# A projection with rotary embedding: when stores are issued, and two more tile pairs that take the block path

## The chip, the cores and the metric

The kernel runs on one core of one Trainium2 chip. The time is device microseconds of one execution of the whole program; lower is better. A profile is one further execution, with the hardware profiler on.

## The reference

`x` is 16 x 512 x 768, `weight` 768 x 768, `cos` and `sin` 512 x 64, all float32; there are 12 heads of 64.

```python
y = np.matmul(x, weight)
y = y.reshape(batch, seq, n_heads, head_dim)
y1, y2 = y[..., :head_dim // 2], y[..., head_dim // 2:]
...
out1 = y1 * cos1 - y2 * sin1
out2 = y2 * cos2 + y1 * sin2
out = np.concatenate([out1, out2], axis=-1)
```

So it is one matrix product of 8192 rows by 768 x 768, and on each head a rotation by the row's position. 25.17 MB of `x` are read and 25.17 MB of `out` written.

## The kernel before, in words

**Tiles and groups.** The rows are cut into 64 tiles of 128 rows, and these into 16 groups of 4 tiles. A group takes the rows of one residue of the position modulo 4 from four batches, so that one slice of cos and sin serves it. A group's result, 128 x 3072, is computed in PSUM in three units of 1024 columns (two banks each, six banks in all), which cut across the tiles: unit 0 is done a third into the group's second tile, unit 1 two thirds into the third, unit 2 at the end of the fourth. The last two groups use units of 512 or 256 columns.

**A tile's way.** TensorE needs the tile's x transposed, in float16. There are two ways:

- *Plain*: SP loads 384 KB (`load`, L189), ScalarE casts it (`cast`, xc<-xs), TensorE transposes six 128 x 128 chunks into PSUM, and ScalarE copies them out (`turn`, L232 and xt<-pt).
- *Block*: two neighbouring tiles, a pair (g, 0) or (g, 1) of group g, are loaded as four quarters of 192 KB (`load_quarter`, L201), quarters 0 and 1 by SP and 2 and 3 by ScalarE's queue; ScalarE casts the pair in one instruction (`cast_pair`, xd<-xb), and VectorE turns it by one stream transpose (`turn_pair`, L252). TensorE does no transposes for it. `BLOCKS` (L135) names the pairs that go this way: 17 before.

Twelve matmuls (L291) then make the tile's 768 output columns. When a unit of 1024 columns is complete, VectorE multiplies it by cos and by sin in one instruction (`rope`, L309, into one of five product buffers: three `tq`, and two in the space of the raw weights, which the profile calls `w_raw`), and POOL adds the halves into the group's output buffer (L320). There are four output buffers `ov`, so group g + 4 writes where group g's result was.

**What sets the order.** All instructions are put out by one Python loop over the tiles, and each engine runs its own in that order; a small class, `Flow`, adds the semaphore waits that reads and writes call for. A step waits with everything behind it on its engine, and a DMA issue holds its issuing engine in the same way. At tile i the loop (L499 to L522) puts out, in this order: the tile's matmuls, with `rope` after the piece that completes a unit; stream transposes of pairs up to 6 tiles ahead (3 for the first tiles: L511, `SETTLED` is 8); TensorE transposes up to 3 tiles ahead; casts up to 7 tiles ahead (3 or 4 for the first); then a store, if one is due. Within `casts`, ScalarE also issues quarters 2 and 3 of a pair some 12 tiles ahead (`LEAD`, L462), and `pump` gives SP its next loads, in the order of `fetch` (L363 to L366), as long as one of 11 row buffers, or one of 4 pair buffers, is free. A pair's cast goes into one of two buffers xd.

**Stores.** A group's output leaves in two halves of 768 KB. Half 0 of group g - 1 is issued at the first tile of group g, half 1 at the third (L514 to L517): from ScalarE's queue up to group 12, from SP's queue for groups 13 and 14. The last group's output goes in smaller pieces as its adds end.

The functions as they stand:

Of the kernel before, what the change touches and what calls it, by code (L numbers as in the profile page):

```python
# [16 lines left out]
class Flow:  # L17
# [24 lines left out]
    def do(self, e, make, reads=(), writes=(), dma=None, tick=True):  # L42
        need = {}
        for k in reads:
            for s, v in self.wrote.get(k, {}).items():
                need[s] = max(need.get(s, 0), v)
        for k in writes:
            for d in (self.wrote, self.readby):
                for s, v in d.get(k, {}).items():
                    need[s] = max(need.get(s, 0), v)  # L50
        if e == "pe":
            need.pop("pe", None)
        waits = self.settle(e, need)
        for s, v in waits[:-1]:
            self.eng[e].wait_ge(self.sem(s), v)
        i = make(self.eng[e])
        if waits:
            s, v = waits[-1]
            i.wait_op(self.sem(s), v, "sem-ge")
        name, step = (dma, 16) if dma else (e, 1)  # L60
        self.sem(name)
        at = self.count[name] + step
        if tick or dma:
            i.then_inc(self.sems[name], step)
            self.count[name] = at
            self.known[name, at] = dict(self.seen[e])
        for k in reads:
            d = self.readby.setdefault(k, {})
            d[name] = max(d.get(name, 0), at)
        for k in writes:  # L70
            self.wrote[k] = {name: at}
            self.readby[k] = {}
        return i
# [30 lines left out]
def kernel(  # L104
# [15 lines left out]
    B, S, H = x.shape  # L120
# [7 lines left out]
    QB = 4  # L128
# [3 lines left out]
    LAST = NG - 1  # L132


    BLOCKS = {(g, 1) for g in range(3, 15)} | {(g, 0) for g in (5, 7, 9, 11, 13)}  # L135

    def sbuf(name, shape, dt):
        return nc.alloc_sbuf_tensor(name, shape, dt).ap()
# [33 lines left out]
    def where(i):  # L172
        g, s = divmod(i, QB)
        return QB * (g // SB) + s, g % SB

    def pair_of(i):
        return i // QB, (i % QB) // 2

    def is_block(i):
        return pair_of(i) in BLOCKS  # L180

# [63 lines left out]
    def turn_pair(gh):  # L245
        g, h = gh
        z = ring("xp", NXP)
        dst = xp_b[z].bitcast(FP32)
        c = xc[gh]
        src, rd = xd_b[c].bitcast(FP32), [f"xd{c}"]  # L250
        v = xp_b[z].rearrange("p (t m e) -> p t e m", t=NT, e=2)
        do("dve", lambda eng: eng.transpose(out=dst, in_=src), reads=rd, writes=[f"xp{z}"])  # L252
        for s in (0, 1):
            xT[g * QB + 2 * h + s] = (
                lambda t, e, s=s: v[:, t, e, ts(s, P)], f"xp{z}")
# [3 lines left out]
    def units(g):  # L259
        if g < LAST - 1:  # L260
            return [(c, c + 1024, py[:, c : c + 1024], [f"ps{c // 512}", f"ps{c // 512 + 1}"], "pool")
                    for c in (0, 1024, 2048)]
        u = [(c, c + 512, py[:, c : c + 512], [f"ps{c // 512}"], "pool")
             for c in range(0, 3072 if g < LAST else 1536, 512)]
        if g == LAST:
            for k, (home, bank) in enumerate([
                (py[:, 1536:1792], "ps3"), (py[:, 0:256], "ps0"),
                (py[:, 2048:2304], "ps4"), (py[:, 2560:2816], "ps5"),
                (pt_b[0][:, 0:256], "pt0"), (pt_b[1][:, 0:256], "pt1"),
            ]):  # L270
                c = 1536 + 256 * k
                u.append((c, c + 256, home, [bank], "pool" if k < 3 else "dve"))
        return u

    def pieces(g, s):

        out_, lo = [], s * H
        for c0, c1, ps, banks, _ in units(g):
            step = 512 if len(banks) > 1 else c1 - c0
            for k, b in enumerate(banks):  # L280
                a, z = max(lo, c0 + k * step), min(lo + H, c0 + (k + 1) * step)
                if a < z:
                    out_.append((a, z, ps[:, a - c0 : z - c0], b))
        return out_

    def mm_piece(i, piece, c, start, stop, tick):
        g, s = divmod(i, QB)
        a, z, ps, bank = piece
        get, key = xT[i]
        t, h = c  # L290
        do("pe", lambda eng: eng.matmul(  # L291
            ps, get(t, h), w_sb[:, t, h, a - s * H : z - s * H], start=start, stop=stop),
            reads=[key, f"w{t}{h}"], writes=[bank], tick=tick)
# [37 lines left out]
    def store(g, c0, c1, e):  # L331

        o = ov_of[g]
        b, r = where(g * QB)
        s0, s1 = c0 // H, -(-c1 // H)
        dst = out.rearrange("b (p r) h -> r p b h", r=SB)[r, :, b + s0 : b + s1]
        src = ov_b[o].rearrange("p (b h) -> p b h", b=QB)[:, s0:s1]
        if (c1 - c0) % H:
            dst = dst[:, 0, c0 - s0 * H : c1 - s0 * H]
            src = src[:, 0, c0 - s0 * H : c1 - s0 * H]  # L340
        do(e, lambda eng: eng.dma_start(out=dst, in_=src),  # L341
           reads=[f"ov{o}c{c}" for c in range(c0, c1, 64)], dma=f"ov{o}_{c0}")
# [20 lines left out]
    want = [(i, i) for i in range(QB, NTILE) if not is_block(i)]  # L363
    for g, h in BLOCKS:
        want += [(g * QB + 2 * h - 2.5 + 3 * q, ((g, h), q)) for q in (0, 1)]
# [78 lines left out]
    state = {"cast": 4, "turn": 4, "bturn": 0, "half": 0}  # L444
    pairs = sorted(BLOCKS)

    def casts(upto):
        while state["cast"] < min(upto, NTILE):
            i = state["cast"]
            state["cast"] += 1  # L450
            if not is_block(i):
                castx(i, "act")
            elif i % 2 == 0:
                cast_pair(pair_of(i))
                xb_used[0] += 1
            pump()
            if state["half"] < 2 * len(pairs):
                n, q = divmod(state["half"], 2)
                g, h = pairs[n]
                if n < xb_used[0] + NB and i >= g * QB + 2 * h - LEAD:  # L460
                    load_quarter(pairs[n], 2 + q, "act")
                    state["half"] += 1  # L462

    def turns(upto):
        while state["turn"] < min(upto, NTILE):
            i = state["turn"]
            state["turn"] += 1
            if not is_block(i):
                turn(i, "act")

    def bturns(upto):
        while state["bturn"] < len(pairs):
            gh = pairs[state["bturn"]]
            if gh[0] * QB + 2 * gh[1] >= upto:
                return
            turn_pair(gh)
            state["bturn"] += 1

    C_AHEAD, T_AHEAD, B_AHEAD = 7, 3, 6
    LEAD = 12  # L480
    SETTLED = 2 * QB
# [14 lines left out]
    rope(0, U0[2])  # L496
    turns(6)

    for i in range(QB, NTILE):  # L499
        g, s = divmod(i, QB)  # L500
        us = units(g)
        done_to = (s + 1) * H
        for p in pieces(g, s):
            a, z, _, bank = p
            for c in CHUNKS:
                mm_piece(i, p, c, c == CHUNKS[0], c == CHUNKS[-1],
                         tick=c == CHUNKS[-1])
            for u in us:
                if u[1] == z:
                    rope(g, u)  # L510
        bturns(i + (B_AHEAD if i >= SETTLED else 3))  # L511
        turns(i + 1 + (T_AHEAD if i > QB + 1 else 2))
        casts(i + 1 + (C_AHEAD if i >= SETTLED else 3 if i == QB else 4))
        if s == 0 and g > 0:  # L514
            store(g - 1, 0, 2 * H, "sp" if g > LAST - 2 else "act")
        if s == 2 and g > 0:
            store(g - 1, 2 * H, 4 * H, "sp" if g > LAST - 2 else "act")  # L517
        if g == LAST:
            if s == 2:
                store(g, 0, H, "sp")  # L520
            if s == 3:
                store(g, H, 2 * H, "act")  # L522
# [43 lines left out]
```

## Time and profile before

| | us |
|---|---|
| median of 3 runs | 154.24 |
| the 3 runs | 152.16, 154.24, 154.43 |
| the profiled execution, its own time | 152.54 |
| span of the profile, first to last instruction | 150.8 |
| TensorE busy (matmuls and transposes) | 140.7 |
| VectorE busy | 129.1 |
| POOL busy | 112.9 |
| ScalarE busy | 74.8 |
| moved by DMA | 53.11 MB, 352 GB/s over the span |

PE is TensorE, PEld its weight loads, DVE VectorE, ACT ScalarE, POOL GpSimd, SP SyncE; a q behind an engine's name is its queue of DMA issues. In the rows of slices a digit is the busy share of a fortieth of the span in tenths. In the chain of work a row has start, length and the step that the end of the program depended on at that time; x36 counts instructions that were merged. In a wait row the engine, its waiting step and what released it are followed by the total, the number of times and the longest. In the timeline a row has start, length, engine, line, operation, what it writes and reads, shape and count, and in brackets the idle time of the engine before it with what ended it. Stores are ACTq or SPq rows with `out_dram<-ov`, at L341. A DMA issue's row is the time that the queue was held, and not the transfer; for a single issue, the DMA view limited to its moment gives the time to landing.

### The profile page before, as it was taken

What the parts mean: (1) busy time and instruction counts of PE and PEld (TensorE: products, weight loads), DVE (VectorE), ACT (ScalarE), POOL (GpSimd) and SP (SyncE); (2) the same over time, 40 slices, a digit from 0 to 9 for tenths busy, and PEclk for the clock granted to TensorE, in tenths of its full rate; (3) what the DMA queues carried; (4) which work ended last, traced back from release to release, by engine and by line L of the source; (5) the groups of instructions that cost most, each with busy time, mean ns of one, the idle gap of its engine ahead of it and who ended that gap; (6) DMA issues with size and microseconds to landing.
All of it is one profiled execution on the core that took longest, in us unless ns stands there. A gap on an engine that the chain in (4) does not pass through costs nothing.

```text
span 150.8 us, 2454 instructions
## 1 busy us (share of the span) xinstructions
PE 140.7 (93%) x972; PEld 86.9 (58%) x972; DVE 129.1 (86%) x88; ACT 74.8 (50%) x76; POOL 112.9 (75%) x60
## 2 busy tenths in 40 slices
PE   6669999999999999999999999899999999999950
PEld 2335666566666666555665666455666666666740
DVE  0334999677998999999989999899989999998890
ACT  3444778885863380844453372744784408342100
POOL 1000299866897889878989789878988698999970
PEclk9999999999999999999999999999999999999995
DMA  4999999999999999999999999999999999695574
GB/s 129 351 402 398 404 340 286 324 363 303 372 379 406 387 383 378 342 396 390 394 358 399 387 385 390 386 389 391 382 400 406 416 414 397 242 353 216 218 283 153
DMA packets 33147, 53.11 MB, mean 352 GB/s; under 512 B 2288, under 2 KB 20464, under 8 KB 33136
## 3 DMA queue, kind: packets, MB, share of 16 engines
q10 hardware_dynamic: 16752, 27.79, 50.1%
q1 hardware_dynamic: 16384, 25.17, 47.1%
q8 instruction: 7, 0.11, 0.3%
q14 instruction: 4, 0.03, 0.1%
HBM read 27.79 MB, written 25.17 MB: 351 GB/s over the span
## 4 chain that ended last, share of the span: by engine, by line
PE 74%; DVE 6%; ACT 5%; DMA 5%; ACTq 3%; POOL 2%; SPq 1%; issue 1%; DVEq 0%; POOLq 0%
PE py L291 68%; PE pt L232 5%; DMA w_raw<-in_weight_dram 5%; DVE w_raw L309 3%; ACTq L341 2%; ACT xd L169 2%; ACT xc L169 2%; POOL ov L320 2%; ACT xt L169 1%; ACTq L201 1%; DVE xs L309 1%; SPq L189 1%; DVE ov L320 1%; SPq L208 1%; DVE w_sb L169 0%
## 5 line engine op out<-in xcount | busy, mean ns | idle before, releaser
L320 POOL TENSOR_TENSOR ov<-tq 128x1024 f32<-128x1024 f32 (+2 forms) x33 | 69.1, 2109 | 27.9 <-DVE tq L309 27.8
L291 PE MATMUL py<-w_sb,xp 128*128 128x512 f16 (+1 forms) x408 | 69.4, 326 | 0.0
L309 DVE TENSOR_TENSOR tq<-py,csn 128x2048 f32<-128x2048 f32 (+2 forms) x33 | 65.8, 2017 | 4.0 <-PE py L291 3.6
L291 PE MATMUL py<-w_sb,xt 128*128 128x256 f16 (+1 forms) x360 | 61.2, 322 | 2.2 <-DVE w_sb L169 1.6
L291 PEld LDWEIGHTS py<-w_sb,xp 128*128 128x128 f16 x408 | 39.3, 98 | 24.6
L291 PEld LDWEIGHTS py<-w_sb,xt 128*128 128x128 f16 x360 | 33.9, 98 | 24.4 <-DVE w_sb L169 3.1
L320 POOL TENSOR_TENSOR ov<-w_raw 128x1024 f32<-128x1024 f32 (+2 forms) x21 | 43.6, 2086 | 4.6 <-DVE w_raw L309 4.5
L309 DVE TENSOR_TENSOR w_raw<-py,csn 128x2048 f32<-128x2048 f32 (+2 forms) x21 | 42.0, 1998 | 2.7 <-PE py L291 2.0
L169 ACT COPY xt<-pt 128x768 f16<-128x768 f16 x28 | 22.3, 801 | 32.9 <-PE pt L232 26.7
L169 ACT CAST xc<-xs 128x768 f16<-128x768 f32 x30 | 26.2, 903 | 20.6 <-issue 8.3
L169 ACT CAST xd<-xb 128x1536 f16<-128x1536 f32 x17 | 27.7, 1628 | 10.9 <-DVE xp L252 5.2
L252 DVE STREAM_TRANSPOSE xp<-xd 128x768 f32<-128x768 f32 x17 | 16.4, 966 | 1.1 <-ACT xd L169 1.0
L232 PE MATMUL pt<-ident,xc 128*128 128x128 f16 x180 | 15.0, 219 | 0.9 <-ACT xc L169 0.9
L232 PEld LDWEIGHTS pt<-ident,xc 128*128 128x128 f16 x180 | 12.2, 98 | 5.7 <-ACT xc L169 2.5
L169 DVE CAST w_sb<-w_raw 128x768 f16<-128x768 f32 x6 | 3.4, 560 | 4.2 <-DMA w_raw<-in_weight_dram 4.1
L394 PE MATMUL py<-cold 128*128 128x512 f16 x12 | 4.3, 513 | 1.4 <-DVE cold L345 1.4
L169 DVE COPY xt<-pt 128x768 f16<-128x768 f16 x2 | 1.1, 558 | 4.8 <-PE pt L232 4.8
L394 PEld LDWEIGHTS py<-cold 128*128 128x128 f16 x12 | 1.4, 127 | 3.3 <-issue 1.8
L169 ACT ACT_TABLE_LOAD x1 | 1.3, 1283 | 0.9 <-SPq L114 0.9
L291 PE MATMUL pt<-w_sb,xt 128*128 128x256 f16 x12 | 1.5, 272 | 0.0
L309 DVE TENSOR_TENSOR xs<-pt,csn 128x512 f32<-128x512 f32 x2 | 1.3, 682 | 0.0
L291 PEld LDWEIGHTS pt<-w_sb,xt 128*128 128x128 f16 x12 | 1.2, 98 | 0.1
(11 smaller groups left out, 3.4 us busy)
## 6 DMA issues: line engine op xcount, KB each, us to landing
out_dram<-ov ACTq DMA_DIRECT2D x26, 768.0 KB, 13.5
xs<-in_x_dram SPq DMA_DIRECT2D x30, 384.0 KB, 10.4
xb<-in_x_dram SPq DMA_DIRECT2D x34, 192.0 KB, 9.0
xb<-in_x_dram ACTq DMA_DIRECT2D x34, 192.0 KB, 10.7
out_dram<-ov SPq DMA_DIRECT2D x4, 768.0 KB, 3.4
w_raw<-in_weight_dram SPq DMA_DIRECT2D x6, 384.0 KB, 7.4
out_dram<-ov SPq DMA_DIRECT2D x1, 384.0 KB, 2.3
out_dram<-ov ACTq DMA_DIRECT2D x1, 384.0 KB, 2.3
```

The source lines that it names most:

```text
L169: eng.copy(out=o, in_=i_) if e == "act" else eng.tensor_copy(out=o, in_=i_)
L189: do(e, lambda eng: eng.dma_start(out=xs_b[k], in_=x[b].rearrange("(p r) h -> r p h", r=SB)[r]), writes=[f"xs{k}"], dma=f"xs{k}")
L201: do(e, lambda eng: eng.dma_start(out=dst[ts(q, R)], in_=src[r, q]), writes=[f"xb{k}q{q}"], dma=f"xb{k}")
L208: do(e, lambda eng: eng.dma_start(out=w_raw[:, t, h], in_=wv[t, h]), writes=[f"wr{t}{h}"], dma=f"w{t}{h}")
L232: do("pe", lambda eng: eng.transpose(pt[:, t, h, :], src[:, t, h, :], ident), reads=[f"xc{c}", "ident"], writes=[f"pt{k}"], tick=(t, h) == ...
L252: do("dve", lambda eng: eng.transpose(out=dst, in_=src), reads=rd, writes=[f"xp{z}"])
L291: do("pe", lambda eng: eng.matmul(ps, get(t, h), w_sb[:, t, h, a - s * H : z - s * H], start=start, stop=stop), reads=[key, f"w{t}{h}"], w ...
L309: do("dve", lambda eng: eng.tensor_tensor(out=tq.rearrange("p j (h d) -> p j h d", d=D), in0=ps.rearrange("p (h d) -> p h d", d=D) .unsque ...
L320: do(adder, lambda eng: eng.tensor_tensor(out=ov_b[o][:, ds(c0, w)].rearrange("p (h t d) -> p h t d", t=2, d=HD), in0=tq[:, 0].rearrange(" ...
L341: do(e, lambda eng: eng.dma_start(out=dst, in_=src), reads=[f"ov{o}c{c}" for c in range(c0, c1, 64)], dma=f"ov{o}_{c0}")
L394: do("pe", lambda eng: eng.matmul(py[:, ts(b, 512)], cold[:, 0:P], cold, start=True, stop=warmed[0] < WARM - 6), reads=["cold"], writes=[f ...
```

## The change

Three edits. `BLOCKS` gains the pairs (2, 1) and (3, 0), that is tiles 10, 11, 12 and 13: nineteen pairs. The stores of groups 0 to 10 are put out at the first and third tile of the second group after them instead of the next one; the four halves of groups 11 and 12 at the four tiles of group 13; groups 13 and 14 as before. The queue that issues each stays what it was. And at tile 8 the stream transposes look 3 tiles ahead instead of 6: the cast of (3, 0) is put out only after that point, at the end of tile 8.

```diff
-    BLOCKS = {(g, 1) for g in range(3, 15)} | {(g, 0) for g in (5, 7, 9, 11, 13)}
+    BLOCKS = {(g, 1) for g in range(2, 15)} | {(g, 0) for g in (3, 5, 7, 9, 11, 13)}
...
+    STORES = {}
+    for o in range(LAST):
+        for k in (0, 1):
+            if o < LAST - 4:
+                at = QB * (o + 2) + 2 * k
+            elif o < LAST - 2:
+                at = QB * (LAST - 2) + 2 * (o - LAST + 4) + k
+            else:
+                at = QB * (o + 1) + 2 * k
+            STORES[at] = (o, k)
...
-        bturns(i + (B_AHEAD if i >= SETTLED else 3))
+        bturns(i + (B_AHEAD if i > SETTLED else 3))
         turns(i + 1 + (T_AHEAD if i > QB + 1 else 2))
         casts(i + 1 + (C_AHEAD if i >= SETTLED else 3 if i == QB else 4))
-        if s == 0 and g > 0:
-            store(g - 1, 0, 2 * H, "sp" if g > LAST - 2 else "act")
-        if s == 2 and g > 0:
-            store(g - 1, 2 * H, 4 * H, "sp" if g > LAST - 2 else "act")
+        if i in STORES:
+            o, k = STORES[i]
+            store(o, 2 * H * k, 2 * H * (k + 1), "sp" if o > LAST - 3 else "act")
```

## The prediction

> **What bounds the kernel now.** I read the page's engine rows first, then its slices, then the chain of work that ended last, then the timeline at the two places that the change touches, and the DMA view by stretches.
>
> ```profile
> PE 140.7 (93%) x972; PEld 86.9 (58%) x972; DVE 129.1 (86%) x88; ACT 74.8 (50%) x76; POOL 112.9 (75%) x60
> PEclk9999999999999999999999999999999999999995
> DMA  4999999999999999999999999999999999695574
> ```
>
> TensorE is busy 93% of the span at a granted clock of 0.99, and the DMA engines are as full until slice 34. So either could be the limit; the chain decides.
>
> ```profile
> 44.03 13.65 PE py L291 x84
> 57.68 0.34 PE pt L232 x6
> 58.01 1.95 PE py L291 x12
> ...
> 84.15 2.37 POOL ov L320
> 86.53 1.23 ACTq L341
> ...
> 92.18 1.67 ACTq L341
> 93.85 0.04 issue
> 93.89 0.80 ACT xt L169
> 94.69 1.51 ACT xd L169
> ...
> 96.63 0.81 ACT xt L169
> 97.43 0.05 issue
> 97.48 9.92 PE py L291 x60
> ```
>
> From about 11 us to 143 us the chain is TensorE back to back: 13.65 / 7 = 1.95 us for a tile's 12 matmuls and 0.34 us (0.335 between tile starts) more after each tile that is followed by six transposes. It leaves TensorE once. There a store on ScalarE's queue waits for POOL's add, its issue and a later one take 1.23 and 1.67 us, and the copy of tile 41's xT behind them comes late: that tile starts 2.58 us after tile 40, 0.63 more than 1.95. Tile 33 starts 2.18 after tile 32, 0.23 too late, for the same queue. All other steps from tile 13 to 61 are within 0.02 us of 1.95 or 2.285.
>
> The waits of ScalarE between 44 and 118 us show how its in-order queue is held by stores:
>
> ```profile
> ACT xc L169 <- issue: 8.3, 3, 3.7
> ACT xc L169 <- POOL ov L320: 4.9, 2, 2.9
> ACT xd L169 <- issue: 2.3, 2, 1.9
> ```
>
> "issue" is a cast behind a DMA that the queue took long to accept (one store issue took 3.48 us from 69.31).
>
> **The change, part by part.** Its own time is 152.54 us, 150.8 of it span. The three plain runs are 152.16, 154.24 and 154.43; so the profiled one is 1.1% below their median, and I do the sum on it.
>
> *Four tiles lose their TensorE transposes.* Tiles 10 to 13, as pairs (2,1) and (3,0). They were four sets after tiles 7, 8, 9 and 10, where the timeline shows TensorE without a gap:
>
> ```profile
> 28.13 0.50 PE L232 MATMUL pt<-ident,xc 128*128 128x128 f16 x6
> 28.47 2.11 PE L291 MATMUL py<-w_sb,xt 128*128 128x512 f16 x12
> 30.42 0.50 PE L232 MATMUL pt<-ident,xc 128*128 128x128 f16 x6
> 30.75 2.11 PE L291 MATMUL py<-w_sb,xt 128*128 128x256 f16 x12
> ```
>
> 4 x 0.335 = 1.34 us, all on the path: -1.34. Matmuls from xp cost what those from xt cost (379 and 273 ns in both groups): 0.
>
> *ScalarE* loses 4 casts (903 ns) and 4 copies (801 ns) and gains 2 pair casts (1628 ns): 3.6 us less, off the path. *SP* loses four 384 KB loads and gains four 192 KB quarters, so that the rows of tiles 16 and 17 go behind seven quarters instead of three, and they are not cast before ScalarE has cast (3,1); *ScalarE's queue* gains four quarter issues of 0.32 to 0.44 us, under casts already running: 0 while it is ahead. The bytes are equal.
>
> *VectorE* gains two stream transposes, 2 x 0.97 = 1.94 us. Here is the cover:
>
> ```profile
> 28.34 2.29 DVE L309 TENSOR_TENSOR tq<-py,csn 128x2048 f32<-128x2048 f32 x1 [1.30 <-PE py L291]
> 31.61 2.29 DVE L309 TENSOR_TENSOR tq<-py,csn 128x2048 f32<-128x2048 f32 x1 [0.98 <-PE py L291]
> 34.91 0.98 DVE L252 STREAM_TRANSPOSE xp<-xd 128x768 f32<-128x768 f32 x1 [1.00 <-ACT xd L169]
> ```
>
> The edit of the look-ahead at tile 8 puts (3,0)'s transpose to tile 9, beside (3,1)'s. The first new transpose fills 30.63 to 31.60, the idle 0.98 before the rope multiply at 31.61. That multiply ends at 33.8; (3,0) takes 33.7 to 34.7 and (3,1) 34.6 to 35.6, in the place of the idle 1.00 and the old one. The next multiply then starts at 35.5 instead of 35.81: VectorE loses nothing. TensorE needs its banks in time: this multiply ends at 37.8, and TensorE writes those banks again in tile 13, at 39.95 before and 38.6 after. Slack 0.8, cost 0. If the cover is gone, each us beyond it is a us on the path.
>
> *Are the new pairs there in time?* Without transposes tile 10 starts at 28.13 + 2 x 1.95 = 32.03. The transpose must end by then, so the pair's cast (1.63) must start by 29.3. ScalarE's last copy ahead of it ends at 27.2. The last quarter of (2,1) is issued where (3,1)'s is now, at 16.87, which took 13.9 us to land (the DMA view narrowed to this one issue); with that it lands at 30.8, the cast ends at 32.4, the transpose at 33.4, and tile 10 is 1.4 late. For the last quarter of (3,1), now issued at 23.77 in the place of another that took 13.9, the landing would be 37.65; its transpose, which VectorE takes ahead of the multiply, would end at 40.3, that multiply at 42.5, against a need at 38.6 + 1.4: 2.5 more. So this step costs between 0 and 3.9. I take 0: the 13.9 were made while two stores, issued at 22.70 and 26.75, shared the engines, and these now come after ScalarE's cast of (3,1), near 33. By 18.8 us 5.8 MB had landed (four tiles, the weights, cos and sin, tiles 4 to 7); up to the last needed quarter of (3,1) 4.15 MB remain (eight row loads' worth of 0.393 MB less the four landed, 13 quarters of 0.197): 14.6 us at the 285 GB/s of 22.6 to 28.5 us, 10.4 at the 400 of the slices before: 29.2 to 33.4. The cast of (3,1) can't start before 31.6 anyway (its buffer), and VectorE wants it done by 34.6. For (2,1) about 2 MB remain: 23.8 to 25.8.
>
> *Stores one group later.* Every ScalarE store up to group 10 then finds its adds done 8 us earlier; the waits for POOL (4.9 above) go. 1.57 MB, a group's output, is taken out of what is in flight: 4.0 us at the 388 GB/s of 44 to 118 us, against store landings of 12.5 to 15.4 us for those issued from 35 to 100 us. With less in flight the queue should take issues faster. On the path that is worth between 0 and the 0.23 + 0.63 = 0.86 us of tiles 33 and 41. I take 0.63: that one's chain holds the POOL wait itself, tile 33's only slow issues: -0.63.
>
> What is late next: a group's output buffer is used again four groups on. By the landings of before, a store one group later would land up to 1.1 us after POOL wants the buffer (group 12; issue 102.2, landing 118.7, add 117.6), with TensorE 2 us earlier some 3 us. POOL writes from five product buffers, so VectorE feels it only after some 5 x 2.7 - 2.3 - 2.4 = 8.8 us: cost 0, upper end 1. At the end groups 11 and 12 put 3.1 MB into group 13; from 134 us on the DMA share is 0.62 of 16.8 us, 6.4 us free against 4.0: cost 0, upper end 1, since the last store is issued by the last add.
>
> Sum: 152.54 - 1.34 - 0.63 = 150.57, say 150.6.
>
> [...] The slices move up to 416 GB/s, and 388 over 44 to 118 us. [...]
>
> **Rivals.** (a) *Only the transposes count*: the queue stays as full and the two stalls stay. For it: ScalarE holds the same number of DMAs in the same order. Against: 4 us less in flight. 152.54 - 1.34 = 151.2. (b) *The transfers are the limit*: 28.70 MB from 44 to 118 us with every slice at 9; if 388 GB/s is all there is, TensorE waits for what it gained: 152.5. Against: no load is waited for after 16 us, and a deferred group gives 4 us back. (c) *The other side, slower: the first pairs land late.* If (2,1) and (3,1) land as the quarters issued at those times did before: 150.6 + 1.4 + 2.5 = 154.5. For it: 22.6 to 28.5 us is the slowest loading of the run (285 GB/s), and more of it is now in quarters. Against: no store competes. It turns the change into a loss when the last quarter of (3,1) lands after about 35.5, where the lateness passes 1.97.
>
> **How the numbers follow.** The forecast (149.6 to 151.2) has 0.5, (a) 0.2, (b) 0.13, (c) 0.12, and 0.05 is for what I don't see. The range 149.4 to 153.6 takes in all but most of (c) and half of the unseen. 2% is about what a measurement of this kernel can tell from no change. Against the median of 154.24, 2% faster is below 151.2: four fifths of the forecast, less some of it since the comparison may meet runs of before like the profiled one, against which 150.6 is 1.3%: 0.38. Over 157.3 needs (c) with more than before's landings, or something unseen: 0.08. Within: 0.54.
>
> **What would show it.** TensorE: tile steps of 1.95 from tile 8 to 13; tile 41 without its 0.63. VectorE: the transposes at 30.6, 33.7 and 34.6, with no wait for ScalarE's xd of more than a few tenths. ScalarE: no wait for POOL before group 11, store landings near 9 us, short issues. Wrong: TensorE idle at tile 10 or 13, POOL waiting for a store, or new late xT copies.

## The result and the profile after

| | before | after |
|---|---|---|
| median of 4 runs of each, us | 153.20 | 154.25 |
| lowest and highest, us | 152.02, 154.43 | 153.26, 156.72 |
| ratio, 95% interval | | 1.0111 [1.0065, 1.0157] |
| the profiled execution, us | 152.54 | 154.23 |
| its span, us | 150.8 | 152.4 |

The changed kernel is slower by about 1.1%, and the interval leaves out 1. The ratio is made from the undisturbed runs alone, without the longest of each kernel, which is why it isn't the quotient of the two medians.

From the page of after: TensorE's row, the busy share of the DMA engines in 40 slices of 3.81 us, and what they moved in each.

```profile
PE 140.7 (92%) x948; PEld 86.0 (56%) x948; DVE 130.6 (86%) x90; ACT 72.0 (47%) x70; POOL 112.7 (74%) x60
DMA  4999999999999999999999999999999999998674
GB/s 130 331 399 399 340 300 287 278 217 222 224 363 342 361 387 400 353 400 390 391 394 397 388 393 392 395 382 391 390 393 411 415 416 413 414 403 350 247 285 153
```

The same row of before:

```profile
GB/s 129 351 402 398 404 340 286 324 363 303 372 379 406 387 383 378 342 396 390 394 358 399 387 385 390 386 389 391 382 400 406 416 414 397 242 353 216 218 283 153
```

The 24 transposes are gone (x948 for x972). The new thing is the ninth to eleventh slice, 30 to 42 us: the engines are as busy as ever (9), yet they move 217 to 224 GB/s where before had 363, 303 and 372. In this row of after a 9 stands over 217 GB/s and over 416, so the digit says nothing of the rate behind it.

What that does to TensorE stands in the timeline of after from 34 to 51 us:

```profile
35.03 1.59 ACT L169 CAST xd<-xb 128x1536 f16<-128x1536 f32 x1 [3.53 <-DMA xb<-in_x_dram]
36.66 0.98 DVE L252 STREAM_TRANSPOSE xp<-xd 128x768 f32<-128x768 f32 x1 [1.86 <-ACT xd L169]
37.56 2.25 DVE L309 TENSOR_TENSOR tq<-py,csn 128x2048 f32<-128x2048 f32 x1
...
39.87 1.47 PE L291 MATMUL py<-w_sb,xp 128*128 128x512 f16 x6 [1.01 <-DVE tq L309]
...
40.99 1.64 ACT L169 CAST xd<-xb 128x1536 f16<-128x1536 f32 x1 [2.75 <-DMA xb<-in_x_dram]
```

ScalarE waits 3.53 us for the rows of pair (3,1), whose last quarter was issued at 24.02 and landed at 34.95. VectorE waits for that cast, and so does the rope multiply behind the transpose: it starts at 37.56, where the prediction had 35.5. It frees banks that TensorE writes in tile 13, so TensorE stands idle there; the step from tile 13 to 14 is 3.47 us instead of 2.285, 1.18 lost.

Then pair (4,1). The chain of after over the same stretch:

```profile
28.86 0.33 SPq L201
...
29.23 11.68 DMA xb<-in_x_dram
...
40.99 1.65 ACT xd L169
...
43.05 2.07 ACTq L201
...
45.16 1.41 ACTq L341
...
46.61 0.80 ACT xt L169
```

A quarter of (4,1) sits on SP's queue behind one of (5,0), which waits for a pair buffer; it is issued at 29.23 and takes 11.68 us to land. The cast of (4,1) follows it, then issues on ScalarE's queue, of which a quarter's takes 2.07 us and a store's 1.41, and only then the copy that tile 16 needs. Tile 16 starts 1.81 us late and tile 17 another 0.71.

Set against before in the profiled executions: -1.34 (the four transpose sets), +1.18 + 1.81 + 0.71 = +3.70 (new idle time at tiles 13, 16, 17), -0.75 (tile 41 is not late any more and tile 33 by 0.11, for 0.86 before), +0.15 (tile 4 starts at 18.76 for 18.61). That is +1.76; the two executions differ by 1.69.

### The profile page after: what moved, and what is told of

It is laid out like the page before. It is cut to its first block, busy times and chain, and to the rows that moved or that the text cites. A ratio compares the mean times of both kernels' runs of the same rounds, so it can differ in the third digit from the quotient of the medians.

```text
span 152.4 us, 2425 instructions
## 1 busy us (share of the span) xinstructions
PE 140.7 (92%) x948; PEld 86.0 (56%) x948; DVE 130.6 (86%) x90; ACT 72.0 (47%) x70; POOL 112.7 (74%) x60
## 4 chain that ended last, share of the span: by engine, by line
PE 70%; DMA 12%; ACT 6%; ACTq 3%; DVE 3%; SPq 2%; issue 1%; DVEq 0%
PE py L291 66%; DMA xb<-in_x_dram 8%; DMA w_raw<-in_weight_dram 5%; PE pt L232 4%; ACT xd L169 3%; ACTq L201 2%; ACT xt L169 2%; ACT xc L169 1%; DVE xs L309 1%; ACTq L341 1%; SPq L189 1%; DVE ov L320 1%; SPq L208 1%; DVE w_raw L309 0%; DVE w_sb L169 0%
## 5 line engine op out<-in xcount | busy, mean ns | idle before, releaser
L291 PE MATMUL py<-w_sb,xp 128*128 128x256 f16 (+1 forms) x456 | 77.5, 326 | 1.0 <-DVE tq L309 1.0
L291 PEld LDWEIGHTS py<-w_sb,xp 128*128 128x128 f16 x456 | 43.9, 98 | 29.0 <-DVE tq L309 1.3
L291 PE MATMUL py<-w_sb,xt 128*128 128x256 f16 (+1 forms) x312 | 52.5, 322 | 3.6 <-DVE tq L309 1.6
L291 PEld LDWEIGHTS py<-w_sb,xt 128*128 128x128 f16 x312 | 29.4, 98 | 23.1 <-DVE w_sb L169 2.8
L169 ACT CAST xd<-xb 128x1536 f16<-128x1536 f32 x19 | 30.7, 1618 | 21.4 <-DMA xb<-in_x_dram 8.9
L169 ACT COPY xt<-pt 128x768 f16<-128x768 f16 x24 | 19.1, 799 | 29.0 <-PE pt L232 21.2
L169 ACT CAST xc<-xs 128x768 f16<-128x768 f32 x26 | 22.5, 901 | 18.5 <-POOL ov L320 8.7
L252 DVE STREAM_TRANSPOSE xp<-xd 128x768 f32<-128x768 f32 x19 | 18.4, 967 | 2.1 <-ACT xd L169 1.9
L232 PEld LDWEIGHTS pt<-ident,xc 128*128 128x128 f16 x156 | 10.8, 100 | 4.8 <-ACT xc L169 1.3
L232 PE MATMUL pt<-ident,xc 128*128 128x128 f16 x156 | 13.3, 223 | 0.2 <-ACT xc L169 0.2
## 6 DMA issues: line engine op xcount, KB each, us to landing
out_dram<-ov ACTq DMA_DIRECT2D x26, 768.0 KB, 13.5
```

What stands on the lines that cost most here:

```text
L169: eng.copy(out=o, in_=i_) if e == "act" else eng.tensor_copy(out=o, in_=i_)
L232: do("pe", lambda eng: eng.transpose(pt[:, t, h, :], src[:, t, h, :], ident), reads=[f"xc{c}", "ident"], writes=[f"pt{k}"], tick=(t, h) == ...
L291: do("pe", lambda eng: eng.matmul(ps, get(t, h), w_sb[:, t, h, a - s * H : z - s * H], start=start, stop=stop), reads=[key, f"w{t}{h}"], w ...
```

## The experiments

Two theories of why the quarters land late stood at the outset: they compete with something else in flight (stores, row loads, the order of issues), or the quarter loads are slow in themselves, by the size of their packets (768 bytes) or by where they write (32 of 128 partitions). In the expectations from experiment 5 on, theory P is the last of these: the partitions set the rate, and two such loads beside each other are hardly faster than one. Ratios are to the kernel before on the same chip.

**1. The pairs alone.** Before, with the new `BLOCKS` and the edit at tile 8; stores as before.

```diff
+    BLOCKS = {(g, 1) for g in range(2, 15)} | {(g, 0) for g in (3, 5, 7, 9, 11, 13)}
...
-        bturns(i + (B_AHEAD if i >= SETTLED else 3))
+        bturns(i + (B_AHEAD if i > SETTLED else 3))
```

> The two new pairs alone; stores as before. Theory Q (the new pairs' quarter loads, 768-byte packets with little else on the engines, move slowly and come late, and SP is held behind them): the stall around tiles 13 to 17 stays, at least as long as the 3.7 us of the changed kernel, since two stores now share the engines at that time: 154 to 156 us. Rival S (the later stores cause it: reads without writes beside them, a POOL that waits): no stall there, and the transposes' 1.34 us are gained: about 151.2 us.

Measured 156.16 against 152.22, ratio 1.0255 [1.0189, 1.0321]. The last quarter of (3,1) lands at 36.43 instead of 34.95, and the steps behind tiles 13, 15 and 16 are 4.78, 4.91 and 3.36 us. The new pairs make the loss, and stores beside them make it larger. The step of 3.36 is not a load's: TensorE is never idle in it, but from 49.66 to 53.07 us its granted clock was 0.5 (in after it stayed at 1.0 until the matmuls were done). The row of 40 slices shows it:

```profile
PEclk9999999999998699999999999999999999999999
```

The stalls of tiles 33 and 41 are gone here too, with the stores of before.

**2. The stores alone.** The seventeen pairs of before with the table `STORES` of after.

```diff
+        if i in STORES:
+            o, k = STORES[i]
+            store(o, 2 * H * k, 2 * H * (k + 1), "sp" if o > LAST - 3 else "act")
```

> The later stores alone; the 17 pairs of before. Theory Q: no early stall; the late starts of tiles 33 and 41 (0.86 us) shrink to about the 0.11 of the changed kernel: 151.8 us, same or slightly faster. Rival S: an early stall of 1 us or more without the new pairs, 153.5 us or more.

Measured 152.14 against 152.22, ratio 0.9986 [0.9949, 1.0024]: no difference. Stores issued from 35 to 100 us land in 13.5 us (median), as before (13.5); the lateness of the steady part sits at tile 33 alone and is 0.72 us (0.86 at tiles 33 and 41 before). From 30 to 42 us this kernel moves 254 GB/s (346 before): with the stores gone from that stretch its rate falls without new pairs too, and nothing is late. Beside early pairs a later store is worth something: about 1.4%, from 1.0255 to 1.0111, of which the half clock of experiment 1 is a part.

**3. The order of two loads.** After, with the two quarters of SP's list swapped that the chain shows.

```diff
+    m, n = fetch.index(((4, 1), 1)), fetch.index(((5, 0), 0))
+    fetch[m], fetch[n] = fetch[n], fetch[m]
```

> The changed kernel with two entries of SP's order exchanged: quarter 1 of pair (4,1) goes ahead of quarter 0 of (5,0), which needs a buffer that is free only after the cast of (2,1). Theory Q with SP held: that quarter is issued near 23.5 instead of 29.2 us and lands by 37, the wait of 2.75 us for it goes, tiles 16 and 17 lose their 2.5 us: about 151.8 us. Rival R (only the rate of the quarters counts, the order merely passes the lateness on): (3,1) or (5,0) gets later by as much, gain under 1 us: 153.3 us or more.

Measured 154.0 against 152.22, ratio 1.0108 [1.0046, 1.017]: as after. The wait for (4,1) fell from 2.75 to 0.93 us, but the issues of ScalarE's queue then took until 46.45, and the copy of tile 16 began at 46.49 (46.61 in after). The order was what the chain showed, and not the cause: lateness taken away at one place came back at the next, and the rate of the stretch stayed low (237 GB/s from 30 to 42 us).

**4. Larger packets.** After, but a quarter takes whole rows of 3072 bytes into the same 32 partitions.

```diff
-        src = x[b : b + 2].rearrange("b (j a r) (q k) -> r q a (b j) k", r=SB, a=R, q=NQ)
+        src = x[b : b + 2].rearrange("b (j a r) h -> r j a b h", r=SB, a=R)
...
-        dst = xb_b[k].rearrange("p (j k) -> p j k", j=2 * NQ)
+        dst = xb_b[k].rearrange("p (b h) -> p b h", b=2)
```

> The changed kernel with each quarter load taking whole rows of x (3072-byte packets) instead of quarters of rows (768 bytes) into the same 32 partitions, the same bytes; the product then mixes up columns, so its numbers are not the reference's. If the packets' size sets the slow stretch from 30 to 42 us (225 GB/s): 340 GB/s or more there, no wait for xb, all of the 3.7 us gone: about 150.5 us. If the order and the number of the loads set it: still over 153 us.

**5. All partitions.** After, but each quarter writes all 128 partitions, in packets of 1536 bytes.

```diff
+        src = x[b + q // 2].rearrange("(p r) h -> r p h", r=SB)[r][:, ts(q % 2, H // 2)]
...
+        dst = xb_b[k][:, ts(q, H // 2)]
```

> The changed kernel with every quarter load writing all 128 partitions (half rows, 1536-byte packets, the same 192 KB) instead of 32; the product mixes up columns. [...] By P the stretch from 30 to 42 us moves 330 GB/s or more, no cast waits for xb, and the time is 150 to 151 us. Rival G (reads without stores beside them are slow by themselves, or the gathering of rows is): 225 GB/s stays, 153 us or more.

**6. Half of the partitions.** After, but each quarter writes partitions 0 to 63 or 64 to 127, in packets of 3072 bytes.

```diff
+        src = x[b + q % 2].rearrange("(p r) h -> r p h", r=SB)[r][ts(q // 2, 64)]
...
+        dst = xb_b[k][ts(q // 2, 64), ts(q % 2, H)]
```

The question is whether the rate of the quarter loads goes with the number of partitions that a load writes.

> As the run before, with 64 partitions for each load (0 to 63 for quarters 0 and 1, 64 to 127 for 2 and 3; whole rows, 3072-byte packets); the product mixes up columns. [...] If it goes with the number of partitions: near 400 GB/s and about 151 us.

The three are read together. They move the same bytes but put columns of `x` in the wrong places, so they are probes of the transfers and no candidates. The row of 30 to 42 us of each kernel: window, length, busy us (and instructions) of PE, PEld, DVE, ACT, POOL, then the granted clock, the DMA share and GB/s. After:

```profile
30.00:42.00 12.00, 10.99 (x73) 6.59 (x72) 10.14 (x7) 5.71 (x5) 6.84 (x3) 1.00 1.12 225
```

Whole rows into 32 partitions:

```profile
30.00:42.00 12.00, 12.00 (x67) 6.69 (x66) 10.28 (x7) 6.49 (x5) 5.56 (x3) 0.89 1.04 229
```

Half of the partitions:

```profile
16.00:28.00 12.00, 11.79 (x94) 7.62 (x95) 10.28 (x6) 9.91 (x12) 11.04 (x5) 1.00 1.04 287
30.00:42.00 12.00, 12.00 (x83) 7.45 (x82) 11.86 (x8) 5.20 (x5) 9.64 (x5) 1.00 1.04 305
```

All partitions:

```profile
16.00:28.00 12.00, 11.79 (x96) 7.54 (x94) 10.30 (x6) 10.11 (x14) 10.70 (x5) 1.00 1.05 386
30.00:42.00 12.00, 12.00 (x83) 7.39 (x82) 11.87 (x9) 7.09 (x6) 9.59 (x5) 1.00 1.01 353
```

Four times larger packets leave the rate where it was: 229 for 225 GB/s, and 221 in both from 34 to 42 us, where after moves almost nothing but quarters (1.71 of 1.77 MB). On SP's queue a packet of 3072 bytes then takes 220 ns (median of 30 to 42 us, by the trace's packet records), against 121 ns for a row's in after's steady part. So the size is not the cause. The time of this kernel, 156.26 against 152.22, ratio 1.0226 [1.0159, 1.0293], says nothing of it, for it is lost elsewhere: the rows of tile 9 take 16.92 us to land, so that the step from tile 6 to 7 is 4.94 us (3.02 in after), and from 29.28 to 32.69 us the granted clock is 0.5, which stretches the next two steps to 2.97 and 2.62; from tile 9 on no tile is late.

```profile
PEclk9999999779999999999999999999999999999996
```

With 128 partitions, at half that packet size, the rate is 386 GB/s from 16 to 28 us, the last quarter of (3,1) lands at 30.11, no cast waits for a quarter, and the time is 149.78 against 152.0: ratio 0.9844 [0.9787, 0.99]. So of the two properties it is the partitions that a load reaches: from 30 to 42 us 229 GB/s with packets of 3072 bytes into 32 of them, and 353 with packets of 1536 bytes into 128.

With 64 neighbouring partitions the rate is 287 in that same window, like after's 302 and far from 386, but 305 from 30 to 42 us, between the two. Casts wait 4.4 us for quarters, yet TensorE loses only 0.64 us, at tile 17, of the 3.70 of after. The time, 153.68 against 152.0, ratio 1.0085 [1.004, 1.013], is lost at the end: from the start of tile 61 to the end of the span it takes 15.1 us (11.6 in after), because POOL waits for stores to land. From the waits of 100 to 152 us:

```profile
POOL ov L320 <- DMA out_dram<-ov: 6.2, 3, 4.1
```

So 64 neighbours do less than 128; how far they are better than 32 stays open.

But 32 partitions do not fix the rate. In after SP's quarters write partitions 0 to 63 and ScalarE's 64 to 127. From 23 to 25 us quarters alone, 0.37 MB in SP's queue and 0.29 in ScalarE's, moved 329 GB/s; from 34 to 42 us, almost alone, 221; and SP's queue alone moved 239 from 63 to 66 us of experiment 10, all of it quarters. So quarters in two queues moved at times no more than those in one, and at times 1.4 times as much; why was not tested.

**7. One new pair.** After without (2,1): eighteen pairs.

```diff
-    BLOCKS = {(g, 1) for g in range(2, 15)} | {(g, 0) for g in (3, 5, 7, 9, 11, 13)}
+    BLOCKS = {(g, 1) for g in range(3, 15)} | {(g, 0) for g in (3, 5, 7, 9, 11, 13)}
```

> The changed kernel without pair (2,1): 18 pairs, (3,0) the new one, stores later. Theory P: half of the added quarters (0.79 MB instead of 1.57), so half of the 3.7 us of stall or less, against 0.67 us of transposes saved: 152 to 153 us, the same as before or slightly slower. Rival (what costs is the first pair that TensorE needs early, (2,1)): no stall, 151.4 us.

Measured 152.62 against 152.0, ratio 1.0035 [0.9992, 1.0079]. The rate from 30 to 42 us is 266 GB/s, little over the 254 of experiment 2 without new pairs; the loss at tile 13 is gone, but tiles 17 and 33 are late by 0.27 and 0.65 us, and the two transpose sets saved (0.67 us) don't show in the time. With half the extra quarters the change is no longer shown to be a loss.

**8. The pairs where loads have room.** Seventeen pairs and (14,0), (15,0), with the later stores.

```diff
+    BLOCKS = {(g, 1) for g in range(3, 15)} | {(g, 0) for g in (5, 7, 9, 11, 13, 14, 15)}
```

> The later stores with two other new pairs, (14,0) and (15,0), at the end instead of (2,1) and (3,0). Theory P: at that time stores go out beside the quarters and TensorE's loads are far ahead, so the four sets of transposes are saved without a stall: 152.1 - 1.34 = 150.8 us. Rival (the quarters or VectorE's two more transposes cost as much there): 152 us or more.

Measured 152.23 against 152.0, ratio 1.0002 [0.9962, 1.0043]. The four sets are gone and nothing stalls: TensorE's last stretch on the chain ends at 140.85, for 143.26 before. Yet the span shrinks only from 150.8 to 150.2. From the chain of this kernel, its end:

```profile
138.98 1.87 PE py L291 x17
...
141.34 1.28 DVE tq L309 x2
...
145.01 1.65 DVE ov L320 x3
```

From TensorE's end to VectorE's last add it takes 5.8 us here, 3.9 before (143.26 to 147.20). VectorE is busy 35.31 of the 36 us from 110 to 146 (33.95 before), and POOL adds without a gap from 127.88 to 145.71. The gain of TensorE meets two engines that are full.

**9 to 11. Does ScalarE's queue matter?** All four quarters issued by SP; once on after, once on the stores of after with seventeen pairs, once on before.

```diff
-        want += [(g * QB + 2 * h - 2.5 + 3 * q, ((g, h), q)) for q in (0, 1)]
+        want += [(g * QB + 2 * h - 2.5 + 0.75 * q, ((g, h), q)) for q in range(NQ)]
...
-            if state["half"] < 2 * len(pairs):
-                n, q = divmod(state["half"], 2)
-                g, h = pairs[n]
-                if n < xb_used[0] + NB and i >= g * QB + 2 * h - LEAD:
-                    load_quarter(pairs[n], 2 + q, "act")
-                    state["half"] += 1
```

> The changed kernel (19 pairs, later stores) with all four quarters of a pair issued by SP, in the order of need; ScalarE's queue issues only stores. If two quarter loads beside each other are hardly faster than one (theory P), SP alone loads as fast as both, and ScalarE is no longer held by slow issues: the waits for issue (5 us) go, tiles 16 and 17 start on time, and only the late landing of (3,1) is left: about 152 us. [...]

> The same with the 17 pairs of before and the later stores. Theory P: no early stall, none at tiles 33 and 41 either (0.86 us): about 151.2 us, and no wait of ScalarE for issue. [...]

> The kernel before with nothing changed but that all quarters are issued by SP. If the later stores have no use of their own, as the stores-only run says (0.999): the same as the run with later stores within 0.5%. If ScalarE's waits for POOL ahead of its stores matter once its queue is otherwise free: 1 us more than with later stores.

All three are much slower: 163.3, 161.47 and 163.17 against 152.08, ratios 1.072 [1.0667, 1.0774], 1.0606 [1.0555, 1.0657] and 1.0714 [1.066, 1.0769]. From the waits of the second of them (later stores, seventeen pairs) over its whole run:

```profile
ACT xd L169 <- DMA xb<-in_x_dram: 31.2, 15, 4.5
ACT xc L169 <- DMA xs<-in_x_dram: 26.0, 16, 3.3
```

Loads are late all through the run. Two things are seen. SP's 47 load issues from 35 to 100 us hold it for 60.0 of these 65 us (31 issues and 13.8 us before), so a load is issued late; and it lands later after that: quarters in 10.7 us (7.9 from SP's queue and 10.2 from ScalarE's before) and rows in 11.7 (9.3), while stores land in 8.3 us (13.5 in before). With the stores through sooner, the loads run by themselves at times, and then near the low rate of experiment 4: the 239 GB/s from 63 to 66 us. With all loads in one queue and the stores in another, the stores gain and the loads lose: ScalarE's share of the quarter issues, which looks like a burden on a busy queue, is worth more than it costs. Which of the two things counts for how much was not separated, and the profile of each kernel also has a stretch of 3.41 us at a granted clock of 0.5 (that of the third has two). How the two queues share the DMA engines was not shown. Between the last two, 1.0606 and 1.0714, later stores look worth 1%, but the one stretch of half clock more is of that size too.

**12. Pairs in the middle.** Before, with (6,0) and (10,0) added.

```diff
+    BLOCKS = {(g, 1) for g in range(3, 15)} | {(g, 0) for g in (5, 6, 7, 9, 10, 11, 13)}
```

> The kernel before with two more pairs in the middle, (6,0) and (10,0), and its own stores and queues. There stores go out beside the quarters (386 GB/s), and VectorE has about 0.45 us to spare in every eight tiles, with 1.7 us of slack on the PSUM banks. If the early place was what cost the changed kernel its gain: four sets of transposes less, 152.1 - 1.34 = 150.8 us. [...]

Measured 151.52 against 151.84, ratio 0.9979 [0.9949, 1.0009]: not shown to be faster. No load holds TensorE up, the stalls of tiles 33 and 41 are gone, and TensorE's last stretch on the chain ends at 141.63 (143.26). But the chain of this kernel now goes over VectorE twice:

```profile
95.84 2.29 DVE w_raw L309
98.13 0.89 DVE xp L252
99.02 2.18 DVE tq L309
101.19 0.47 DVE xp L252
...
144.58 2.06 DVE ov L320 x3
```

With twelve tiles in a row on the block path, groups 9 to 11, and a stream transpose (0.97) between most multiplies, VectorE is busy 13.87 of the 14 us from 92 to 106 (13.45 before) and 35.23 of the 36 from 110 to 146. Its end comes 0.56 us earlier, not 1.63.

No version tried here that computes the reference is shown to beat the kernel before. A load in the layout of the block path that reaches all partitions in one transfer was not tried.

## Why the prediction was wrong, point by point

- **"Are the new pairs there in time? ... I take 0"** is the step that failed. It took 4.15 MB at 285 to 400 GB/s and got 29.2 to 33.4 us; the last quarter of (3,1) landed at 34.95. Both rates were read in stretches of before in which row loads made about half of the bytes (the slower) or nearly all (the faster). The bytes were right and their kind was not: 13 quarters (2.56 MB) at the 225 GB/s of after's slow stretch take 11.4 us, 1.57 MB of rows at 400 take 3.9, and 18.8 + 15.3 = 34.1, near the landing. (After moved 266 GB/s on average from 18.8 to 34.95 us.) Experiments 4 and 5 show that the size of the packets did not set that rate (229 GB/s with 3072 bytes) and that loads into all partitions ran faster in the same stretch (353). It is no fixed rate of these loads either: from 23 to 25 us of after they moved 329 GB/s.
- **"The 13.9 were made while two stores ... shared the engines"**, the reason for taking 0, was a misreading of the issue times. By the packet records of before, the first store's packets move from 28.07 us on; by then 11.2 of the 13.9 us of the quarter issued at 16.87 were over, and the slowest stretch, 22.6 to 28.5 us at 285 GB/s, had next to no store in it. In after no store packet moves before 41.66 us, and a packet of 768 bytes takes longer there (61 ns, median of 30 to 42 us) than in that stretch of before (52).
- **The same step had one place, and there were two.** It looked at tiles 10 and 13. Of the 3.70 us lost, 2.52 came at tiles 16 and 17, through pair (4,1), which is no new pair: it is loaded in the same stretch, behind the extra quarters, and the copy for tile 16 then waits for slow issues on ScalarE's queue as well.
- **Rival (c)**, "the first pairs land late", given 0.12, was the mechanism and its 154.5 is near the profiled 154.23. In part by chance: (2,1), whose 1.4 us were in it, was in time; (3,1) cost 1.18 for its 2.5; and (4,1) was not in it. Its turning point, "after about 35.5" for that landing, counted only the first place; with 34.95 the change is a loss already.
- **"With less in flight the queue should take issues faster ... -0.63"** failed. The stores alone change nothing (0.9986), and their landings stay at 13.5 us. In after the two stalls of the steady part did shrink from 0.86 to 0.11, but they also vanish with the pairs alone (experiment 1) and with the middle pairs (12), and with the stores alone most of it stays (0.72, experiment 2). So that gain was booked under the wrong edit; which of the pairs' effects removes the stalls was not settled. The waits that were read as ScalarE waiting for POOL did not go either. From the waits of after between 44 and 118 us:

```profile
ACT xc L169 <- POOL ov L320: 8.7, 3, 3.1
```

  The adds that these stores read were long done (the store issued at 72.12, a half of group 4, reads adds that ended by 61.6), so what such a row measures is the queue's slow acceptance of an issue (the two quarter issues ahead of this store took 2.12 us), put down to POOL because a store names it.
- **Four tiles lose their transposes, -1.34:** right. The steps from tile 7 to 13 are 1.95 us each.
- **VectorE has room:** right where the data were there. The transposes of (2,1) and (3,0) ran at 30.77 and 33.84 (forecast 30.6 and 33.7); the third was to start at 34.6 and started at 36.66, for want of its cast.
- **POOL waits for store landings, hidden:** right; 2.8 us in three waits, the longest 1.7, and VectorE does not feel them. **The tail costs nothing:** right; from TensorE's end to VectorE's last add it is 3.94 us in both.
- **"The transfers are the limit"**, rival (b), "if 388 GB/s is all there is": after's slices go to 416 GB/s, and with all partitions reached the kernel moved 404 GB/s from 42 to 110 us and kept the whole gain (every tile step 1.95 or 2.285 from tile 7 on). The limit was local, in one stretch and for one kind of load.

## What to carry to other kernels

Price a moved load by the rate of its own kind, measured where little else runs, and not by the mean rate of a stretch: a busy DMA row can hide a transfer at half speed (a 9 for 217 GB/s and for 416 here). Issue times don't tell what runs beside a load; the packets do (the store issued at 22.70 us in before moved its first packet at 28.07). Read the granted clock and the place of the loss before a time is put down to the edit. When a few loads become late, look for every consumer in the same stretch, old ones too, and try the rate before the order. And where one engine is relieved in a kernel whose engines are all nearly full, put the relief where the next engine still has gaps, or it is given back at the end.

## What the runs showed of the hardware that was not expected

- From 30 to 42 us loads into 32 partitions ran at 225 GB/s in packets of 768 bytes (after, DMA share 1.12) and at 229 in packets of 3072 (experiment 4, 1.04); 64 neighbouring partitions gave 305 there, and 287 from 16 to 28 us, with row loads and stores beside them. Loads into 128 partitions alone moved 402 from 8 to 15 us of before. But loads into 32, alone, moved 329 from 23 to 25 us of after; what makes the difference was not tested.
- A packet of 768 bytes took 61 ns (median) from 30 to 42 us of after, and 36 from 44 to 110 us, beside stores and rows, where the whole moved 386 GB/s: there the slowness of these loads hardly shows.
- Taking half of the quarter loads off the queue that also carries the stores, and giving them to the queue of all other loads, made the kernel 6 to 7% slower: in experiment 10 SP's issues held it for 60.0 of 65 us, and loads landed later (quarters in 10.7 us for 7.9 to 10.2, rows in 11.7 for 9.3).
- The granted clock fell to 0.5 for 3.41 us in the midst of experiments 1, 4 and 9 to 11, and not in before or after; what brings it on was not tested.
